# Weights of both half-steps in a permuted column order in SBUF, read back in order by TensorE, and split 512 columns at a time

## The chip, the cores and the metric

The kernel runs on one core of one Trainium2 chip. The metric is the device time of one execution in microseconds (us), shown as the median of the runs. A profiled execution has a span of its own, from its first to its last instruction. The core's engines work side by side, each through its own list of instructions: TensorE (PE; the loading of its stationary operand is shown apart as PEld), VectorE (DVE), ScalarE (ACT), GpSimd (POOL), and SyncE (SP), whose queue issues the loads of the weights.

## The reference, cut to what matters

One decoder layer for 256 tokens of 2048 features: a SwiGLU half-step, a mixer of three branches, a second SwiGLU half-step and a final norm, in float32.

```python
D_MODEL, SEQ, D_FF = 2048, 256, 5632

def swiglu(h, w_gate, w_up, w_down):
    return (jax.nn.silu(h @ w_gate) * (h @ w_up)) @ w_down

x = x + 0.5 * swiglu(rmsnorm(x, ffn1_norm[l]), ffn1_w_gate[l], ffn1_w_up[l], ffn1_w_down[l])
x = x + mixer(rmsnorm(x, mix_norm[l]), mem_n, ...)
x = x + 0.5 * swiglu(rmsnorm(x, ffn2_norm[l]), ffn2_w_gate[l], ffn2_w_up[l], ffn2_w_down[l])
return rmsnorm(x, final_norm)
```

w_gate and w_up are 2048 x 5632, w_down is 5632 x 2048. The mixer's weights lie between them in time.

## The kernel before, in words

Every matrix product with a weight goes through `gemm` (line 127). It makes a 128-token by 512-column result for each of the two blocks of tokens (`NB` = 2, `CW` = 512), and walks the rows of the weight in feature tiles of 128. `load` (line 106) brings four feature tiles with one DMA of 1 MB from the SP queue into a buffer `raw`, of which there are three. `split` (line 118) takes two of the four tiles at a time, 1024 columns in one instruction on each engine: ScalarE copies them, rounded to the type float32r, to `wh` (line 119), and VectorE subtracts `wh` from `raw` into `wl` (line 120), so that the two parts sum up to the weight. `wh` and `wl` have three buffers each. The activations are split in the same way (class `Split`). `products` (line 122) then issues three products for a feature tile and a block, into the same accumulator: high by high (line 123), high activation by low weight (line 124), low activation by high weight (line 125). In all three the activation is the stationary operand of 128 columns and the weight tile the moving operand, 512 columns of 4 bytes that lie one behind the other in SBUF.

Two feature tiles, called a pair below, are thus one split on each engine and 2 tiles x 2 blocks x 3 products = 12 products.

`ffn` (line 309) is a half-step. It works in two parts, of 6 and 5 chunks of 512 hidden features. A chunk is a `gemm` with w_gate over 16 feature tiles, a Silu on ScalarE, a `gemm` with w_up over 16 feature tiles, the product of both on VectorE, and its transposition and split (`tsplit`). Behind the chunks of a part come four `gemm`s with w_down, over 24 and over 20 feature tiles. `ffn` is called at line 402 for the first half-step and at line 784 for the second, with the mixer between them. In the very last `gemm` of the second half-step the last two groups of four tiles are split ahead into other buffers and taken block by block (`tail=2`).

Small pieces of other work (norms, masks, attention) are threaded between the products by `tick`. The order of the instructions on each engine is set by a scheduler that simulates a timeline of the program as it is built. Lines 653 and 654, in the mixer's linear attention, are VectorE subtractions on a view of 1024 columns cut in groups of 2m, of which one instruction takes the first m columns of each group and the other the last m, for m = 64, 32, 16, 8, 4, 2 and 1. One of their inputs is a single column of each group, repeated.

Of the kernel before, what the change touches and what calls it, by code (L numbers as in the profile page):

```python
# [8 lines left out]
F32 = mybir.dt.float32  # L9
# [4 lines left out]
ALU = mybir.AluOpType  # L14
AX = mybir.AxisListType
PSUM = bass.MemoryType.PSUM

P = 128
# [3 lines left out]
KT = D // P  # L22
DFF = 5632
CW = 512
NCH = D // CW
EPS = 1e-6
# [7 lines left out]


class Split:
    """A transposed activation [features, tokens] as two exact float32r parts, 8 feature tiles to a
    slot: x = high + low, each with at most 12 significant bits."""

    def __init__(self, new, n_tiles):  # L40
        n = (n_tiles + 7) // 8
# [18 lines left out]
def layer(ctx: ExitStack, tc: tile.TileContext, a: dict, out: bass.AP):  # L60
    nc = tc.nc
# [24 lines left out]
    x0 = a["x"][0]  # L86
    mem0 = a["mem"][0]

# [1 line left out]
    queue = []  # L90

    def tick(n=1):
# [9 lines left out]
        while queue and (gen is None or gen in queue):  # L102
            tick()

# [1 line left out]
    def load(w, row, col, parts=1):  # L106
        """Four feature tiles of a weight; parts: DMAs."""
        raw = wp.tile([P, 4, CW], F32, name="raw", tag="raw")
        n = 4 // parts
        for i in range(0, 4, n):  # L110
            r = row + i * P
            nc.sync.dma_start(
                raw[:, i : i + n, :],
                w[r : r + n * P, col : col + CW].rearrange("(j p) n -> p j n", p=P),
            )
        return raw

    def split(raw, wh, wl):
        nc.scalar.copy(wh, raw)  # L119
        nc.vector.tensor_tensor(wl, raw, wh.bitcast(F32), op=ALU.subtract)  # L120

    def products(lhs, kt, b, wh, wl, acc, first, last):
        nc.tensor.matmul(acc, lhsT=lhs.h(kt, b), rhs=wh, start=first, stop=False)  # L123
        nc.tensor.matmul(acc, lhsT=lhs.h(kt, b), rhs=wl, start=False, stop=False)  # L124
        nc.tensor.matmul(acc, lhsT=lhs.l(kt, b), rhs=wh, start=False, stop=last)  # L125

    def gemm(lhs, n_tiles, w, row0, col0, accs, ticks=0, raws=(), tail=0):
        """accs[b] = lhs of block b times a [n_tiles * P, CW] part of w. The last `tail` groups of
        four feature tiles go block by block, so that the first block is done early."""
        raws = list(raws)  # L130
        held = []
        for g0 in range(0, n_tiles, 4):
            raw = raws.pop(0) if raws else load(w, row0 + g0 * P, col0)
            late = g0 >= n_tiles - 4 * tail
            if late:
                both = [slot([P, 4, CW], F32R) for _ in range(2)]
                held.append((g0, *both))
            for h0 in (0, 2):
                if late:
                    wh, wl = (t[:, h0 : h0 + 2, :] for t in both)  # L140
                else:
                    wh = wp.tile([P, 2, CW], F32R, name="wh", tag="wh")
                    wl = wp.tile([P, 2, CW], F32R, name="wl", tag="wl")
                split(raw[:, h0 : h0 + 2, :], wh, wl)
                if late:
                    continue
                for b in range(NB):
                    for j in range(2):
                        kt = g0 + h0 + j
                        products(  # L150
                            lhs, kt, b, wh[:, j, :], wl[:, j, :], accs[b],
                            kt == 0, kt == n_tiles - 1,
                        )
                tick(ticks)
        for b in range(NB):
            for g0, wh, wl in held:
                for j in range(4):
                    kt = g0 + j
                    products(
                        lhs, kt, b, wh[:, j, :], wl[:, j, :], accs[b], kt == 0, kt == n_tiles - 1  # L160
                    )
# [12 lines left out]
        nc.scalar.copy(hi, ps)  # L174
        nc.vector.tensor_tensor(lo, ps, hi.bitcast(F32), op=ALU.subtract)  # L175

# [1 line left out]
    def square(src, ss, b, n):  # L178
        junk = tmp()
        nc.scalar.activation(junk, src, AF.Square, accum_out=ss[:, b, n : n + 1])  # L180
# [13 lines left out]
            )  # L194

    def rsqrt_mean(out_ap, sum_ap, n):
        """out = (sum / n + EPS) ** -0.5"""
        w = sum_ap.shape[1]
        t = sp.tile([P, 8], F32, name="rs", tag="rs")
        nc.vector.tensor_scalar(  # L200
            out=t[:, :w], in0=sum_ap, scalar1=1.0 / n, scalar2=EPS, op0=ALU.mult, op1=ALU.add
        )
        nc.gpsimd.tensor_tensor(out_ap, t[:, :w], mhalf[:, :w], op=ALU.pow)  # L203
# [9 lines left out]
            cp.tile([P, NB], F32, name=f"rs_{name}"),  # L213
        )

# [1 line left out]
    ident = cp.tile([P, P], F32, name="ident")  # L217
    make_identity(nc, ident)
    mhalf = cp.tile([P, 8], F32, name="mhalf")
# [10 lines left out]
        nc.tensor.transpose(out=ps[:, :n], in_=src, identity=ident[:n, :n])  # L230
        nc.vector.tensor_copy(gT[:, rows], ps[:, :n])

# [1 line left out]
    ss_m, rs_m = stats("m")  # L234
    mem_s = [slot([P, NB, 2 * CW]) for _ in range(2)]
    memT = Split(slot, KT)
# [4 lines left out]
    first = []  # L241
    for n in range(NCH):
        part = mem_s[n // 2][:, :, n % 2 * CW : (n % 2 + 1) * CW]
# [10 lines left out]
    xT = Split(slot, KT)  # L254
# [33 lines left out]
    for c in range(4):  # L288
        accs = [acc() for _ in range(NB)]
# [5 lines left out]
        for b in range(NB):  # L295
            r = rs_m[:, b : b + 1]
            if c < 2:
                t = tmp()
# [6 lines left out]
                )  # L305
    drain()

# [1 line left out]
    def ffn(xT, rs, wg, wu, wd, after, begin=lambda: None, final=False):  # L309
        done = 0  # L310
        for part, n_ch in enumerate((6, 5)):
            hT = Split(slot, 4 * n_ch)
            for c in range(n_ch):
                col = (done + c) * CW
                pg = [acc() for _ in range(NB)]
                gemm(xT, KT, wg, 0, col, pg, ticks=1)
                sil = [tmp() for _ in range(NB)]
                for b in range(NB):
                    nc.scalar.activation(sil[b], pg[b], AF.Silu, scale=rs[:, b : b + 1])  # L319
                pu = [acc() for _ in range(NB)]  # L320
                gemm(xT, KT, wu, 0, col, pu, ticks=1)
                for b in range(NB):
                    nc.vector.scalar_tensor_tensor(  # L323
                        out=sil[b], in0=pu[b], scalar=rs[:, b : b + 1], in1=sil[b],
                        op0=ALU.mult, op1=ALU.mult,
                    )
                    tsplit(sil[b], hT, 4 * c, b)
            if part == 1:
                begin()
            for n in range(NCH):  # L330
                pd = [acc() for _ in range(NB)]
                ends = final and part == 1 and n == NCH - 1
                gemm(
                    hT, 4 * n_ch, wd, done * CW, n * CW, pd, ticks=1, tail=2 if ends else 0
                )
                for b in range(NB):
                    xs = x_s[b][:, n * CW : (n + 1) * CW]
                    nc.vector.scalar_tensor_tensor(  # L338
                        out=xs, in0=pd[b], scalar=0.5, in1=xs, op0=ALU.mult, op1=ALU.add
                    )  # L340
                    if part == 1:
                        after(xs, b, n)
            done += n_ch
# [5 lines left out]
        nonlocal xT2  # L349
        xT2 = Split(slot, KT)  # L350

# [1 line left out]
    # acc[s, t] of a level m takes s in the first and t in the second half of a block of 2m.  # L353
    LEVELS = (64, 32, 16, 8, 4, 2, 1)
    masks = cp.tile([P, 8, P], U8, name="masks")
    tri = cp.tile([P, P], F32, name="tri")
# [3 lines left out]
    def prepare():  # L360
# [6 lines left out]
            out=masks[:, 7, :], in0=ix, scalar1=0, scalar2=None, op0=ALU.is_equal  # L367
        )
        yield
        at = tp.tile([P, 4, P], F32, name="at", tag="tmp")  # L370
        for i, m in enumerate(LEVELS):
            nc.vector.scalar_tensor_tensor(
                out=at[:, 0, :], in0=ix, scalar=m, in1=lt, op0=ALU.is_ge, op1=ALU.mult
            )
            nc.vector.scalar_tensor_tensor(
                out=masks[:, i, :], in0=ix, scalar=2 * m, in1=at[:, 0, :],
                op0=ALU.is_lt, op1=ALU.mult,
            )
        yield
        # Cumulative sums by a triangle, with GLA_TAU's exact 1/16.  # L380
        nc.gpsimd.memset(tri, 1.0 / 16.0)
        nc.gpsimd.affine_select(
            out=tri, in_=tri, pattern=[[1, P]], compare_op=ALU.is_ge, fill=0.0,
# [6 lines left out]
            out=ws, in_=ws, pattern=[[0, 4], [-1, P]], compare_op=ALU.is_ge, fill=0.0,  # L390
# [11 lines left out]
    def to_mixer(xs, b, n):  # L402
# [4 lines left out]
        xT, rs_1, a["ffn1_w_gate"][0], a["ffn1_w_up"][0], a["ffn1_w_down"][0],  # L407
        to_mixer,
        begin_mixer,
    )  # L410
    drain()
    for b in range(NB):
        rstd_of(ss_2, rs_2, b)

# [1 line left out]
    w_in = a["w_in"][0]  # L416
    rq = cp.tile([P, NB], F32, name="rq")
    nc.vector.tensor_scalar_mul(rq, rs_2, DK ** -0.5)
# [7 lines left out]
            for b in range(NB):  # L426
                leave(c, b, accs[b])

    # low-rank gate, [rank, tokens]
    glr = cp.tile([RANK, S], F32, name="glr")  # L430
    graw = tp.tile([P, KT, RANK], F32, name="graw", tag="tmp")
    nc.sync.dma_start(
# [16 lines left out]
                )  # L449
        nc.vector.tensor_copy(glr, pg[:RANK, :S])  # L450

    # spatial gating
    su = slot([P, NB, BW])
    sv = slot([P, NB, BW])

# [60 lines left out]

    queue.append(spatial())

    # cross-attention into the memory
    xqT = slot([P, 8, S])  # L520

    def to_T(dst_of, r):
# [58 lines left out]

    queue.append(attend())

    # gated linear attention
    qkT = slot([P, 2, HEADS, S])
    v_s = slot([P, NB, BW])
    r_s = slot([P, NB, BW])
    cum = slot([P, 2, HEADS, S])
    def log_decay():
        """cum[:, 0] = running sums of log_sigmoid(gate) / GLA_TAU over each 128 tokens, [d, h, t]"""  # L590
        zz = slot([P, 2, NB, CW])
        bias = tmp()
        bcast(bias, a["gla_gate_bias"][0])
# [10 lines left out]
        z, e = zz[:, 0], zz[:, 1]  # L604
# [21 lines left out]
    def linear_attention():  # L626
# [4 lines left out]
        c, e = cum[:, 0], cum[:, 1]  # L631
# [17 lines left out]
        for i, m in enumerate(LEVELS):  # L649
# [10 lines left out]
            yield  # L660
            level(qk[:, 0], qk[:, 1], i)
            yield
        # between the two blocks of 128
        mid = c[:, :, P - 1 : P].to_broadcast([P, HEADS, P])
        nc.vector.tensor_tensor(e[:, :, :P], mid, c[:, :, :P], op=ALU.subtract)
        nc.scalar.activation(e[:, :, :P], e[:, :, :P], AF.Exp)
# [53 lines left out]
    gla_gen = linear_attention()  # L720
    queue.append(gla_gen)

    # gates and branches
    merged = [slot([P, D]) for _ in range(NB)]
    w_br = a["w_branch"][0]
    for i in (1, 2, 0):
# [34 lines left out]
    for b in range(NB):  # L761
        rstd_of(ss_3, rs_3, b)

# [1 line left out]
    ss_4, rs_4 = stats("4")  # L765
    gf = slot([P, D])
    bcast(gf, a["final_norm"])
# [1 line left out]
    def last(xs, b, n):  # L769
# [12 lines left out]
            nc.sync.dma_start(out[0, b * P : (b + 1) * P, i * CW : (i + 1) * CW], xi)  # L782

    ffn(
        xT3, rs_3, a["ffn2_w_gate"][0], a["ffn2_w_up"][0], a["ffn2_w_down"][0], last, final=True
    )


# [29 lines left out]
```

## Time and profile before

| | |
|---|---|
| median of 2 runs | 2394.95 us (2394.32 to 2395.57) |
| span of the profiled execution | 2393.2 us |
| TensorE busy | 2373.6 us (99%), 10746 matmuls |
| VectorE busy | 1268.2 us (53%) |
| ScalarE busy | 1070.7 us (45%) |
| GpSimd busy | 58.4 us (2%) |
| DMA | 451.76 MB, mean 189 GB/s |

The span is the time of one profiled execution and is compared with another span; the median is that of the unprofiled runs. Matmuls are pipelined, so that the durations of neighbours overlap and a busy TensorE is not TensorE at its peak: what one costs is read from the distance of the starts.

### The profile page before, as it was taken

Reading aid. Unit: us, or ns where it says so; the run is one execution under the profiler, and the core shown is the slowest. Engines: PE = TensorE matmul, PEld = TensorE weight load, DVE = VectorE, ACT = ScalarE, POOL = GpSimd, SP = SyncE. Lnnn points to the kernel's source line nnn. Section 1 sums busy time; section 2 is a strip of 40 time slices with the busy share of each in tenths; the row PEclk is TensorE's granted clock in tenths of the full one; section 3 lists DMA queues with packets and bytes.
Section 4 is the critical chain, followed back from the end, with each engine's and each line's share of the span. In section 5 each row is a group of like instructions: output and inputs, shape, how many; then the busy total and the mean of one; then the engine's idle time right before and its main releaser. Section 6 shows DMA issues by size and latency. Waiting matters only on the chain.

```text
span 2393.2 us, 26429 instructions
## 1 busy us (share of the span) xinstructions
PE 2373.6 (99%) x10746; PEld 1962.7 (82%) x10746; DVE 1268.2 (53%) x1330; ACT 1070.7 (45%) x1265; POOL 58.4 (2%) x56
## 2 busy tenths in 40 slices
PE   8999999999999999999999999999999999999998
PEld 6888888888888878888788888888888888888887
DVE  5644545445545545556765555555454454454454
ACT  6544444344444444435444444445444433444443
POOL 0000000000000001000200000000000000000000
PEclk9999999999999999999999999999999999999999
DMA  7555555566556665445556555555556555556654
GB/s 261 184 191 187 186 193 193 194 193 191 180 192 202 203 195 178 157 163 167 165 164 216 193 194 189 199 192 183 188 192 194 188 188 194 192 187 193 193 189 146
DMA packets 226227, 451.76 MB, mean 189 GB/s; under 512 B 9316, under 2 KB 9384, under 8 KB 225464
## 3 DMA queue, kind: packets, MB, share of 16 engines
q1 hardware_dynamic: 224408, 442.69, 57.0%
q0 software_dynamic: 1696, 7.37, 0.8%
q8 instruction: 84, 1.38, 0.2%
q14 instruction: 39, 0.32, 0.0%
HBM read 445.84 MB, written 4.19 MB: 188 GB/s over the span
## 4 chain that ended last, share of the span: by engine, by line
PE 96%; DVE 1%; ACT 1%; issue 1%; DMA 1%; SPq 0%; ACTq 0%; POOLq 0%; POOL 0%; DVEq 0%
PE acc L124 31%; PE acc L125 31%; PE acc L123 31%; PE trp L166 2%; DVE wl L120 1%; PE sml L638 0%; DMA graw<-in_w_in_dram 0%; PE sml L543 0%; PE sml L571 0%; ACT wh L119 0%; PE sml L446 0%; DMA m<-in_mem_dram 0%; ACT m L655 0%; ACT tmp L180 0%; PE sml L692 0%
## 5 line engine op out<-in xcount | busy, mean ns | idle before, releaser
L120 DVE TENSOR_TENSOR wl<-raw,wh 128x1024 fp32r<-128x1024 f32 x828 | 1028.6, 1243 | 1025.1 <-ACT wh L119 1024.9
L119 ACT CAST wh<-raw 128x1024 fp32r<-128x1024 f32 x828 | 871.3, 1053 | 1158.9 <-PE acc L125 1142.8
L124 PE MATMUL acc<-wl,m 128*128 128x512 f32 x3312 | 1294.9, 391 | 1.9 <-DVE wl L120 1.7
L125 PE MATMUL acc<-wh,m 128*128 128x512 f32 x3312 | 1291.3, 390 | 0.1
L123 PE MATMUL acc<-wh,m 128*128 128x512 f32 x3312 | 1185.8, 392 | 3.5 <-ACT wh L119 2.5
L123 PEld LDWEIGHTS acc<-wh,m 128*128 128x128 f32 x3312 | 622.3, 188 | 133.3 <-ACT wh L119 3.7
L124 PEld LDWEIGHTS acc<-wl,m 128*128 128x128 f32 x3312 | 622.9, 188 | 132.2 <-DVE wl L120 3.6
L125 PEld LDWEIGHTS acc<-wh,m 128*128 128x128 f32 x3312 | 622.5, 188 | 128.1 <-DVE m L191 0.5
L190 ACT ACTIVATE m<-trp,gT 128x128 fp32r<-128x128 f32 x128 | 42.8, 363 | 23.9 <-PE trp L166 14.3
L174 ACT CAST m<-trp 128x512 fp32r<-128x512 f32 x64 | 34.9, 588 | 40.9 <-PE trp L166 40.9
L175 DVE TENSOR_TENSOR m<-trp,m 128x512 fp32r<-128x512 f32 x64 | 41.7, 685 | 21.2 <-ACT m L174 20.9
L191 DVE SCALAR_TENSOR_TENSOR m<-trp,gT,m 128x128 fp32r<-128x128 f32 x128 | 41.1, 346 | 14.3 <-ACT m L190 13.5
L166 PEld LDWEIGHTS trp<-ident,tmp 128*128 128x128 f32 x288 | 34.7, 140 | 6.6
L166 PE MATMUL trp<-ident,tmp 128*128 128x128 f32 x288 | 40.0, 272 | 0.0
L319 ACT ACTIVATE tmp<-acc,rs 128x512 f32<-128x512 f32 x44 | 30.1, 690 | 19.5 <-PE acc L125 19.5
L180 ACT ACTIVATE tmp<-m 128x512 f32<-128x512 f32 x40 | 24.8, 624 | 15.6 <-DVE m L338 11.9
L323 DVE SCALAR_TENSOR_TENSOR tmp<-acc,rs,tmp 128x512 f32<-128x512 f32 x44 | 30.9, 743 | 0.0
L166 PE MATMUL trp<-ident,m 128*128 128x128 f32 x160 | 22.8, 280 | 3.0 <-DMA m<-in_mem_dram 3.0
L338 DVE SCALAR_TENSOR_TENSOR m<-acc,m 128x512 f32<-128x512 f32 x32 | 20.6, 682 | 9.5 <-PE acc L125 9.5
L203 POOL TENSOR_TENSOR rs<-rs,mhalf 128x1 f32<-128x1 f32 x8 | 4.3, 552 | 868.6 <-DVE rs L200 868.6
L166 PEld LDWEIGHTS trp<-ident,m 128*128 128x128 f32 x160 | 19.7, 145 | 6.7 <-DMA m<-in_mem_dram 3.1
L658 POOL TENSOR_TENSOR m<-m,m 128x1024 f32<-128x1024 f32 x7 | 20.9, 2990 | 115.4 <-ACT m L655 88.2
(135 smaller groups left out, 387.3 us busy)
## 6 DMA issues: line engine op xcount, KB each, us to landing
raw<-in_w_in_dram SPq DMA_DIRECT2D x96, 1024.0 KB, 5.0
raw<-in_ffn_w_gate_dram SPq DMA_DIRECT2D x88, 1024.0 KB, 5.2
raw<-in_ffn_w_up_dram SPq DMA_DIRECT2D x88, 1024.0 KB, 5.2
raw<-in_ffn_w_down_dram SPq DMA_DIRECT2D x88, 1024.0 KB, 5.1
raw<-in_w_branch_dram SPq DMA_DIRECT2D x24, 1024.0 KB, 5.1
raw<-in_w_out_dram SPq DMA_DIRECT2D x16, 1024.0 KB, 5.1
raw<-in_w_kv_mem_dram SPq DMA_DIRECT2D x14, 1024.0 KB, 5.1
m<-in_mem_dram SPq DMA_DIRECT2D x4, 512.0 KB, 8.3
```

What stands on the lines that cost most here:

```text
L119: nc.scalar.copy(wh, raw)
L120: nc.vector.tensor_tensor(wl, raw, wh.bitcast(F32), op=ALU.subtract)
L123: nc.tensor.matmul(acc, lhsT=lhs.h(kt, b), rhs=wh, start=first, stop=False)
L124: nc.tensor.matmul(acc, lhsT=lhs.h(kt, b), rhs=wl, start=False, stop=False)
L125: nc.tensor.matmul(acc, lhsT=lhs.l(kt, b), rhs=wh, start=False, stop=last)
L166: nc.tensor.transpose(out=ps[:, j * P : (j + 1) * P], in_=src[:, j * P : (j + 1) * P], identity=ident)
L174: nc.scalar.copy(hi, ps)
L175: nc.vector.tensor_tensor(lo, ps, hi.bitcast(F32), op=ALU.subtract)
L190: nc.scalar.activation(dst.h(kt, b), pj, AF.Copy, scale=g)
L191: nc.vector.scalar_tensor_tensor(out=dst.l(kt, b), in0=pj, scalar=g, in1=dst.h(kt, b).bitcast(F32), op0=ALU.mult, op1=ALU.subtract,)
L319: nc.scalar.activation(sil[b], pg[b], AF.Silu, scale=rs[:, b : b + 1])
L323: nc.vector.scalar_tensor_tensor(out=sil[b], in0=pu[b], scalar=rs[:, b : b + 1], in1=sil[b], op0=ALU.mult, op1=ALU.mult,)
```

## The change

The two calls of `ffn` get three run lengths each: e = 2, 4 and 16 columns for w_gate, w_up and w_down of the first half-step, 32, 64 and 8 for those of the second. For these weights the 512 columns of a feature tile lie in SBUF in another order. A group of 2e columns is cut in two; its first e columns go to the first half of the tile's row (256 columns, 1 KB), its last e columns to the second half, and the next group follows behind. ScalarE and VectorE write `wh` and `wl` through that view, one feature tile (512 columns) per instruction instead of two, and TensorE reads the moving operand through the same view, which gives the columns back in their own order: e columns of one half, e of the other, the next e of the first half, and so on. `raw` is read in order. All other products, the mixer's and the tail's, stay as they were, and so do all loads.

```diff
+    def laid(t, e):
+        if e is None:
+            return t
+        return t.rearrange("p (h c e) -> p c h e", h=2, e=e)
+
-    def split(raw, wh, wl):
-        nc.scalar.copy(wh, raw)
-        nc.vector.tensor_tensor(wl, raw, wh.bitcast(F32), op=ALU.subtract)
+    def split(raw, wh, wl, e=None):
+        if e is None:
+            nc.scalar.copy(wh, raw)
+            nc.vector.tensor_tensor(wl, raw, wh.bitcast(F32), op=ALU.subtract)
+            return
+        for j in range(raw.shape[1]):
+            r = raw[:, j, :].rearrange("p (c h e) -> p c h e", h=2, e=e)
+            hi, lo = laid(wh[:, j, :], e), laid(wl[:, j, :], e)
+            nc.scalar.copy(hi, r)
+            nc.vector.tensor_tensor(lo, r, hi.bitcast(F32), op=ALU.subtract)
...
-                split(raw[:, h0 : h0 + 2, :], wh, wl)
+                split(raw[:, h0 : h0 + 2, :], wh, wl, None if late else e)
...
-                            lhs, kt, b, wh[:, j, :], wl[:, j, :], accs[b],
+                            lhs, kt, b, laid(wh[:, j, :], e), laid(wl[:, j, :], e), accs[b],
...
-                gemm(xT, KT, wg, 0, col, pg, ticks=1)
+                gemm(xT, KT, wg, 0, col, pg, ticks=1, e=runs[0])
...
-                gemm(xT, KT, wu, 0, col, pu, ticks=1)
+                gemm(xT, KT, wu, 0, col, pu, ticks=1, e=runs[1])
...
+                    e=runs[2],
...
+        runs=(2, 4, 16),
...
+        runs=(32, 64, 8),
```

The instructions on ScalarE where the first w_gate chunk of the first half-step ends and its w_up chunk has begun, before (`wh` and `raw` with their buffer numbers):

```order
L119 CAST wh_1131<-raw_1129 128x1024
L119 CAST wh_1147<-raw_1129 128x1024
L119 CAST wh_1171<-raw_1169 128x1024
L119 CAST wh_1187<-raw_1169 128x1024
L319 ACT_TABLE_LOAD
L319 ACTIVATE tmp_1163<-acc_989,rs_1_219 128x512
L319 ACTIVATE tmp_1164<-acc_990,rs_1_219 128x512
L119 CAST wh_1205<-raw_1203 128x1024
```

The same place in the changed kernel, where line 133 is the copy of 512 columns, "128x128x2x2" is 128 partitions by 128 groups of two runs of 2, and "x2" stands for two instructions:

```order
L133 CAST wh_1143<-raw_1141 128x128x2x2 x2
L133 CAST wh_1161<-raw_1141 128x128x2x2 x2
L133 CAST wh_1187<-raw_1185 128x64x2x4 x2
L133 CAST wh_1205<-raw_1185 128x64x2x4 x2
L333 ACT_TABLE_LOAD
L333 ACTIVATE tmp_1179<-acc_989,rs_1_219 128x512
L333 ACTIVATE tmp_1180<-acc_990,rs_1_219 128x512
L133 CAST wh_1225<-raw_1223 128x64x2x4 x2
```

Each copy has become two of half the columns, and the Silu (line 319, now 333) stands at the same place between them; VectorE's subtractions change in the same way.

TensorE in the next w_gate chunk, where the transposes (line 166) of the chunk before come between the products, before:

```order
L123 MATMUL acc_1321<-wh_1341,m8_220 128x512
L124 MATMUL acc_1321<-wl_1342,m8_220 128x512
L125 MATMUL acc_1321<-wh_1341,m8_222 128x512
L124 MATMUL acc_1322<-wl_1342,m8_220 128x512
L125 MATMUL acc_1322<-wh_1341,m8_222 128x512
L166 MATMUL trp_1306<-ident_79,tmp_1163 128x128 x4
L166 MATMUL trp_1314<-ident_79,tmp_1164 128x128 x4
L123 MATMUL acc_1322<-wh_1341,m8_220 128x512
```

And in the changed kernel, where lines 137, 138 and 139 are the three products and line 180 the transposes:

```order
L137 MATMUL acc_1353<-wh_1375,m8_220 128x512
L138 MATMUL acc_1353<-wl_1376,m8_220 128x512
L139 MATMUL acc_1353<-wh_1375,m8_222 128x512
L138 MATMUL acc_1354<-wl_1376,m8_220 128x512
L180 MATMUL trp_1338<-ident_79,tmp_1179 128x128 x4
L180 MATMUL trp_1346<-ident_79,tmp_1180 128x128 x4
L139 MATMUL acc_1354<-wh_1375,m8_222 128x512
L137 MATMUL acc_1354<-wh_1375,m8_220 128x512
```

The transposes have moved ahead of one product; the number and the width of the products are unchanged.

## Rows read from the trace of the kernel before

**Rows 1.** Page, section 1: the span, and busy time of each engine.

```profile
span 2393.2 us, 26429 instructions
PE 2373.6 (99%) x10746; PEld 1962.7 (82%) x10746; DVE 1268.2 (53%) x1330; ACT 1070.7 (45%) x1265; POOL 58.4 (2%) x56
```

**Rows 2.** Page, section 4: chain that ended last, shares by engine and by line.

```profile
PE 96%; DVE 1%; ACT 1%; issue 1%; DMA 1%; SPq 0%; ACTq 0%; POOLq 0%; POOL 0%; DVEq 0%
PE acc L124 31%; PE acc L125 31%; PE acc L123 31%; PE trp L166 2%; DVE wl L120 1%; PE sml L638 0%; DMA graw<-in_w_in_dram 0%; PE sml L543 0%; PE sml L571 0%; ACT wh L119 0%; PE sml L446 0%; DMA m<-in_mem_dram 0%; ACT m L655 0%; ACT tmp L180 0%; PE sml L692 0%
```

**Rows 3.** Grouped lines: operation, shapes, count, busy us, mean ns, idle before, releasers.

```profile
L124 PE MATMUL acc<-wl,m 128*128 128x512 f32 x3312 | 1294.9, 391 | 1.9 <-DVE wl L120 1.7
L125 PE MATMUL acc<-wh,m 128*128 128x512 f32 x3312 | 1291.3, 390 | 0.1
L123 PE MATMUL acc<-wh,m 128*128 128x512 f32 x3312 | 1185.8, 392 | 3.5 <-ACT wh L119 2.5 <-ACT m L190 0.8
L120 DVE TENSOR_TENSOR wl<-raw,wh 128x1024 fp32r<-128x1024 f32 x828 | 1028.6, 1243 | 1025.1 <-ACT wh L119 1024.9
L119 ACT CAST wh<-raw 128x1024 fp32r<-128x1024 f32 x828 | 871.3, 1053 | 1158.9 <-PE acc L125 1142.8 <-issue 12.7 <-ACT m L190 1.0
...
L175 DVE TENSOR_TENSOR m<-trp,m 128x512 fp32r<-128x512 f32 x64 | 41.7, 685 | 21.2 <-ACT m L174 20.9
...
L174 ACT CAST m<-trp 128x512 fp32r<-128x512 f32 x64 | 34.9, 588 | 40.9 <-PE trp L166 40.9
...
L125 PE MATMUL acc<-m,m 128*128 128x512 f32 x16 | 6.2, 389 | 0.0
```

**Rows 4.** Timeline of TensorE, 600 to 606 us: start, duration, operation.

```profile
600.76 0.39 PE L123 MATMUL acc<-wh,m 128*128 128x512 f32 x1
...
603.49 0.39 PE L123 MATMUL acc<-wh,m 128*128 128x512 f32 x1
...
605.98 0.39 PE L125 MATMUL acc<-wh,m 128*128 128x512 f32 x1
```

**Rows 5.** Windows: stretch, length, busy us by engine, granted clock, DMA share, GB/s.

```profile
core 0: us, PE busy (x) PEld busy (x) DVE busy (x) ACT busy (x) POOL busy (x), PEclk, DMA share, GB/s
107.00:486.00 379.00, 379.00 (x1699) 314.35 (x1698) 187.65 (x168) 161.39 (x165) 0.00 (x0) 1.00 0.59 189
...
2032.00:2380.00 348.00, 348.00 (x1558) 288.55 (x1557) 176.18 (x161) 148.02 (x159) 0.00 (x0) 1.00 0.57 184
```

**Rows 6.** Waits: who waited for whom, us in total, times, longest us.

```profile
ACT wh L119 <- PE acc L125: 1142.8, 705, 3.8
...
PE acc L123 <- ACT wh L119: 2.5, 3, 1.7
PE acc L124 <- DVE wl L120: 1.7, 3, 0.9
```

**Rows 7.** Page, section 6: DMA issues, count, KB each, median us to landing.

```profile
raw<-in_ffn_w_gate_dram SPq DMA_DIRECT2D x88, 1024.0 KB, 5.2
...
raw<-in_ffn_w_down_dram SPq DMA_DIRECT2D x88, 1024.0 KB, 5.1
```

**Rows 8.** Timelines of ScalarE and VectorE, 603 to 608 us; in brackets idle time.

```profile
603.68 1.05 ACT L119 CAST wh<-raw 128x1024 fp32r<-128x1024 f32 x1 [1.66 <-PE acc L125]
606.40 1.05 ACT L119 CAST wh<-raw 128x1024 fp32r<-128x1024 f32 x1 [1.67 <-PE acc L125]
...
604.77 1.23 DVE L120 TENSOR_TENSOR wl<-raw,wh 128x1024 fp32r<-128x1024 f32 x1 [1.50 <-ACT wh L119]
```

**Rows 9.** Lines 653 and 654: durations min/median/max in ns, first and last start.

```profile
L653 DVE TENSOR_TENSOR m<-m x7: 678/681/693, 1091.4 to 1198.0; 128x512 f32<-128x512 f32 x7
...
L654 DVE TENSOR_TENSOR m<-m x7: 676/683/686, 1092.0 to 1199.8; 128x512 f32<-128x512 f32 x7
```

**Rows 10.** Timeline of TensorE around line 617, a product of unrounded f32.

```profile
1088.14 1.95 PE L617 MATMUL sml<-tri,m 128*128 128x128 f32 x16
1089.84 0.48 PE L124 MATMUL acc<-wl,m 128*128 128x512 f32 x1
```

More of the change, by code (lines that the diff above doesn't have):

```diff
@@ L125, in products, with gemm @@
         nc.tensor.matmul(acc, lhsT=lhs.l(kt, b), rhs=wh, start=False, stop=last)
-    def gemm(lhs, n_tiles, w, row0, col0, accs, ticks=0, raws=(), tail=0):
+    def gemm(lhs, n_tiles, w, row0, col0, accs, ticks=0, raws=(), tail=0, e=None):
         raws = list(raws)
@@ L306, in layer, with ffn @@
     drain()
-    def ffn(xT, rs, wg, wu, wd, after, begin=lambda: None, final=False):
+    def ffn(xT, rs, wg, wu, wd, after, begin=lambda: None, final=False, runs=(None, None, None)):
         done = 0
@@ L333, in ffn @@
                 gemm(
-                    hT, 4 * n_ch, wd, done * CW, n * CW, pd, ticks=1, tail=2 if ends else 0
+                    hT, 4 * n_ch, wd, done * CW, n * CW, pd, ticks=1, tail=2 if ends else 0,
+                    e=runs[2],
                 )
@@ L784, in layer @@
     ffn(
-        xT3, rs_3, a["ffn2_w_gate"][0], a["ffn2_w_up"][0], a["ffn2_w_down"][0], last, final=True
+        xT3, rs_3, a["ffn2_w_gate"][0], a["ffn2_w_up"][0], a["ffn2_w_down"][0], last, final=True,
+        runs=(32, 64, 8),
     )
```

## The prediction

> **What bounds the kernel now.** I read the page's busy line first: TensorE is busy for 99% of a span of 2393.2 us, VectorE for 53% and ScalarE for 45% [rows 1]. The chain of waits says the same from the other end: 96% of it is TensorE, and three lines, the three products of a split weight, hold 31% each [rows 2]. The grouped lines then give the counts: 3312 instructions on each of these lines, each 512 columns wide, plus 48 in the tail [rows 3]. Their mean of about 390 ns is no price, since they overlap; the price is the spacing of their starts. In the timeline twelve products (one pair of feature tiles, both blocks) go from 600.76 to 603.49 us and 23 of them from 600.76 to 605.98, so one costs 5.22 / 23 = 227 ns, or 0.443 ns a column [rows 4]. [...] Nobody keeps TensorE waiting: it waited 2.5 us in all for ScalarE's wh and 1.7 us for VectorE's wl, while ScalarE waited 1142.8 us for TensorE to give buffers back [rows 6]. So the time follows the spacing of the products, and anything that only burdens the other engines must first use up their idle time.
>
> **What the change does, part by part.**
>
> *Count.* Each half-step has 88 / 2 = 44 loads of each of its three weights [rows 7] (the row of w_up, left out there, reads like that of w_gate); a load is two pairs of feature tiles, so 88 pairs and 88 x 12 = 1056 products for each weight (48 fewer for the last one, whose tail stays as it was). The six weights get runs of e = 2, 4, 16 columns in the first half-step and 32, 64, 8 in the second.
>
> *Splits of 512 columns.* 6 x 88 - 4 = 524 pairs are now split by two instructions on each engine. ScalarE: the 1024-column copy takes 1053 ns, and the nearest 512-column one 588 ns; VectorE: 1243 ns, and 685 ns [rows 3]. A pair then costs 2 x 588 = 1176 ns instead of 1053 on ScalarE and 2 x 685 = 1370 ns instead of 1243 on VectorE: 524 x 123 = 64 us and 524 x 127 = 67 us more work. A pair comes round every 2.72 us, and in it ScalarE idles for 1.67 and VectorE for 1.50 us [rows 8]. That idle time hides both; without it the two sums would be the price. The products wait for no more than before, and the first half of wh is ready sooner. I take 0. The order on TensorE changes only where single products or transposes swap places, which costs nothing while its queue is full.
>
> *Split writes and reads in short runs.* VectorE already does this: lines 653 and 654 each walk 512 of 1024 columns in runs of 64, 32, 16, 8, 4, 2 and 1 with a gap as long as the run, on one input and the output, and all fourteen take between 676 and 693 ns [rows 9]. Runs of 2 are therefore free for VectorE, as far as hops of some bytes stand for hops of 1 KB. For ScalarE no row has such runs. The bounds: nothing, or a doubled price for each column. From 512 to 1024 columns its copy grows by 465 ns, so doubling adds that to each 512: 2 x 1053 = 2106 ns for a pair, still under 2720. If VectorE's halves doubled whole, 2740 ns would pass 2720 by a hair: 88 pairs x some 0.2 us with the work at a chunk's end, under 20 us. I take 0, by the VectorE rows.
>
> *TensorE's reads.* The only term that is not hidden. A product reads 512 columns of wh or wl; now they come as 512 / e runs, taken in turn from the two halves of a 2 KB row. No moving operand of the old kernel is read in runs below 128 columns, so the trace has no row for it. The lower bound is 0 (VectorE's rows: runs of 2 cost nothing there). But TensorE is more pressed: 0.443 ns a column against 685 / 512 = 1.34 ns on VectorE, so 8 adjacent bytes last it 0.89 ns and VectorE 2.7 ns. Whether a pair of columns can be fetched in 0.89 ns from an address that jumps each time is the whole question. [...] For half speed there are two prices. Twice the spacing is 454 ns, 227 more. The nearest slower row of TensorE is line 617: 16 products of 128 columns between 1088.14 and 1089.84 us, 106 ns each, 0.83 ns a column [rows 10]; 512 such columns make 425 ns, 198 more. (Those operands are unrounded f32, so it is a neighbour, not the same thing.) I take the middle, 212 ns: 1056 x 212 = 224 us, with 209 and 239 us at the ends. A gain I exclude: shorter runs cannot beat reading in order, unless today's reading meets some conflict, for which no row speaks.
>
> [...]
>
> **The sum.** 0 + 0 + 224 us on the profiled span of 2393.2 gives 2617; the median shown, 2394.95, lies 1.75 us over that span [rows 1], so 2619 us.
>
> **The rivals.**
>
> *A, reads in order cost nothing from any address:* not slower, 2395 us (2394 to 2400 with leftovers at chunk starts). Place: the 1056 products on ffn1's w_gate. For it speaks that VectorE's fourteen calls do not feel run length at all [rows 9]; against it that TensorE asks for its columns three times as fast. It decides up to 48 us / 1056 = 45 ns for one product: below that the change can't be told from none. [...]
>
> *B, my forecast:* only e = 2 falls to half speed, 2619 us.
>
> *C, longer runs pay too.* Either e = 4 also runs at half speed (a fetch must bring 8 columns): twice the term, 2395 + 448 = 2843 us, or each hop costs the same 212 / 256 = 0.83 ns: (256 + 128 + 32 + 16 + 8 + 64) = 504 hops, 504 x 0.83 x 1056 ns = 442 us, 2837 us. For it speaks that no row shows what a hop of 1 KB costs; against the second that VectorE with 512 hops in 512 columns shows none [rows 9].
>
> *D, e = 2 pays in part,* because fetches overlap: half of the term, 112 us, 2507 us.
>
> *E, ScalarE or VectorE becomes the bound,* priced above: under 20 us and within A, unless a split more than doubles.
>
> **How the numbers follow.** B 0.38, A (with E) 0.35, C 0.15, D 0.10, faster 0.02. [...] The likeliest is 2619 us, its own range 2600 to 2640. A, D and B together are 0.83, so the range goes from 2390 (A) to 2720 (B with up to 45% of the same loss on e = 4); what is left out is most of C. About 2% of 2395, 48 us, is what a measurement of this kernel can tell from no change: slower B, C and nearly all of D, 0.62; same 0.36; faster 0.02.
>
> **What would show it.** In the timeline of the first half-step's w_gate chunks the starts of products should lie 425 to 454 ns apart, and a chunk's 96 products should take 42 us instead of 21.8; with A, 227 ns. In w_up of the same half-step and in all three weights of the second, 227 ns in any case but C. The granted clock stays at 1.00. The split lines show 1048 instructions each, means near 590 and 690 ns whatever e is, and TensorE's waits for wh and wl stay at a few us. I am wrong if the w_gate stretch keeps its 227 ns (A), if the w_up stretch grows as well (C), or if TensorE begins to wait for the splits by tens of us (E).

## The result, and the profile after

The changed kernel takes 2568.88 us (median of 2 runs, 2568.63 to 2569.13) against 2394.95: a ratio of 1.0729, 95% interval 1.0712 to 1.0747. It is 173.9 us slower. The profiled executions differ by as much, 2566.9 against 2393.2 us.

The page of the changed kernel: its span, its busy times and the granted clock of TensorE in 40 slices:

```profile
span 2566.9 us, 27477 instructions
...
PE 2548.7 (99%) x10746; PEld 1978.1 (77%) x10746; DVE 1307.1 (51%) x1854; ACT 1124.5 (44%) x1789; POOL 58.4 (2%) x56
...
PEclk9999999999999999999999999999999999999999
```

TensorE is the bound as before [rows 1, 2], with the same 10746 matmuls, the same granted clock (0.999 in the mean, 0.998 before), and 175 us more of busy time. The grouped lines, which answer to [rows 3] (137 to 139 are the three products, 133 and 134 the halved splits):

```profile
L138 PE MATMUL acc<-wl,m 128*128 128x512 f32 x3312 | 1358.7, 411 | 1.9 <-DVE wl L128 1.8
L139 PE MATMUL acc<-wh,m 128*128 128x512 f32 x3312 | 1356.4, 410 | 0.1
...
L134 DVE TENSOR_TENSOR wl<-raw,wh 128x512 fp32r<-128x512 f32 x1048 | 678.7, 689 | 805.3 <-ACT wh L133 803.8
...
L133 ACT CAST wh<-raw 128x512 fp32r<-128x512 f32 x1048 | 605.7, 626 | 870.6 <-PE acc L139 859.8
```

The products got longer and nothing waits for anything new: the idle time ahead of line 138 is 1.9 us, as it was, ScalarE still waits for TensorE, and VectorE for ScalarE. So the time went into the products themselves. The timeline of TensorE in the changed kernel, one stretch for each run length, in the order of the program: w_gate (e = 2), w_up (4) and w_down (16) of the first half-step, w_up (64), w_gate (32) and w_down (8) of the second:

```profile
190.99 0.51 PE L137 MATMUL acc<-wh,m 128*128 128x512 f32 x1
...
193.32 0.51 PE L139 MATMUL acc<-wh,m 128*128 128x512 f32 x1
...
204.41 0.42 PE L139 MATMUL acc<-wh,m 128*128 128x512 f32 x1
204.67 0.41 PE L137 MATMUL acc<-wh,m 128*128 128x512 f32 x1
204.91 0.42 PE L138 MATMUL acc<-wl,m 128*128 128x512 f32 x1
...
459.69 0.40 PE L137 MATMUL acc<-wh,m 128*128 128x512 f32 x1
...
460.89 0.40 PE L139 MATMUL acc<-wh,m 128*128 128x512 f32 x1
...
1840.03 0.39 PE L137 MATMUL acc<-wh,m 128*128 128x512 f32 x1
...
1841.16 0.39 PE L137 MATMUL acc<-wh,m 128*128 128x512 f32 x1
...
1861.64 0.40 PE L137 MATMUL acc<-wh,m 128*128 128x512 f32 x1
1861.88 0.40 PE L138 MATMUL acc<-wl,m 128*128 128x512 f32 x1
1862.11 0.40 PE L139 MATMUL acc<-wh,m 128*128 128x512 f32 x1
...
2100.54 0.41 PE L137 MATMUL acc<-wh,m 128*128 128x512 f32 x1
...
2101.27 0.65 PE L137 MATMUL acc<-wh,m 128*128 128x512 f32 x2
```

Seven steps from 190.99 to 193.32 us make 333 ns for e = 2. With e = 4 the steps alternate, 0.26 and 0.24 us, 250 ns in the mean. Five steps from 459.69 to 460.89 make 240 ns for e = 16, five from 1840.03 to 1841.16 make 226 for e = 64, the steps of 0.24 and 0.23 at 1861.64 some 236 for e = 32, and three from 2100.54 to 2101.27 make 243 for e = 8. In order it was 227 [rows 4]. Over all products of each weight the mean step is 332, 250, 240, 237, 227 and 243 ns; times 1056 products the six differences, 105 + 23 + 13 + 10 + 0 + 16 = 167 ns, make 176 us, which covers the loss of 173.7 us between the two spans.

### The profile page after: what moved, and what is told of

Same layout as the page of the kernel before. It is cut to its first block, busy times and chain, and to the rows that moved or that the text cites. A ratio compares the mean times of both kernels' runs of the same rounds, so it can differ in the third digit from the quotient of the medians.

```text
span 2566.9 us, 27477 instructions
## 1 busy us (share of the span) xinstructions
PE 2548.7 (99%) x10746; PEld 1978.1 (77%) x10746; DVE 1307.1 (51%) x1854; ACT 1124.5 (44%) x1789; POOL 58.4 (2%) x56
## 4 chain that ended last, share of the span: by engine, by line
PE 97%; DVE 1%; issue 1%; ACT 1%; DMA 1%; ACTq 0%; POOLq 0%; POOL 0%; SPq 0%; DVEq 0%
PE acc L138 31%; PE acc L139 31%; PE acc L137 31%; PE trp L180 2%; PE sml L654 0%; DVE wl L128 0%; DMA graw<-in_w_in_dram 0%; PE sml L559 0%; PE sml L587 0%; PE sml L462 0%; ACT wh L127 0%; ACT m L671 0%; DMA m<-in_mem_dram 0%; ACT tmp L194 0%; PE sml L708 0%
## 5 line engine op out<-in xcount | busy, mean ns | idle before, releaser
L138 PE MATMUL acc<-wl,m 128*128 128x512 f32 x3312 | 1358.7, 411 | 1.9 <-DVE wl L128 1.8
L139 PE MATMUL acc<-wh,m 128*128 128x512 f32 x3312 | 1356.4, 410 | 0.1
L137 PE MATMUL acc<-wh,m 128*128 128x512 f32 x3312 | 1247.6, 411 | 2.3 <-ACT wh L127 1.3
L134 DVE TENSOR_TENSOR wl<-raw,wh 128x512 fp32r<-128x512 f32 x1048 | 678.7, 689 | 805.3 <-ACT wh L133 803.8
L133 ACT CAST wh<-raw 128x512 fp32r<-128x512 f32 x1048 | 605.7, 626 | 870.6 <-PE acc L139 859.8
L128 DVE TENSOR_TENSOR wl<-raw,wh 128x1024 fp32r<-128x1024 f32 x304 | 387.0, 1274 | 332.1 <-ACT wh L127 332.0
L127 ACT CAST wh<-raw 128x1024 fp32r<-128x1024 f32 x304 | 319.0, 1051 | 395.7 <-PE acc L139 386.0
```

Of the source, the lines that this page charges most:

```text
L133: nc.scalar.copy(hi, r)
L134: nc.vector.tensor_tensor(lo, r, hi.bitcast(F32), op=ALU.subtract)
```

## The experiments

Theory R at the start: the cost lies in TensorE's reading and depends on the run length of the read alone. Rival W: it comes from the short-run writes or the doubled number of splits. In the diffs below `+` and `-` stand against the changed kernel, if nothing else is said. In all of its variants but the one with blocks, the two views take the number of parts of a row beside the run length: the changed kernel's own runs then read ((2, 2), (2, 4), (2, 16)) and ((2, 32), (2, 64), (2, 8)), which changes nothing by itself.

**Reads alone.**

```diff
-                split(raw[:, h0 : h0 + 2, :], wh, wl, None if late else e)
+                split(raw[:, h0 : h0 + 2, :], wh, wl)
```

> TensorE reads through the six run lengths (2, 4, 16; 32, 64, 8) as in the changed kernel, but ScalarE and VectorE split 1024 columns at a time in plain order, so the columns that the six products see are in another order (that part of the computation is changed). Theory R, the cost lies in TensorE's reads alone: all of the changed kernel's loss, 2560 to 2575 us, starts of products 333 ns apart in the e = 2 weight, 250 in e = 4, 243 in e = 8, 240 in e = 16, 237 in e = 32, 227 in e = 64. Rival W, the loss comes from the short-run writes or the halved splits meeting TensorE's reads in SBUF: about 2395 us, 227 ns everywhere.

Measured: 2567.81 us, ratio 1.0726 (1.0708 to 1.0744), steps of 331, 250, 240, 237, 227 and 243 ns: the whole loss, with plain writes and 1024-column splits. Its split on ScalarE, and TensorE in the weight with e = 2 (four steps, 333 ns each):

```profile
L127 ACT CAST wh<-raw 128x1024 fp32r<-128x1024 f32 x828 | 872.9, 1055 | 1306.1 <-PE acc L139 1276.7 <-issue 13.3 <-DVE m L353 13.1
```

```profile
190.49 0.51 PE L138 MATMUL acc<-wl,m 128*128 128x512 f32 x1
...
191.82 0.51 PE L139 MATMUL acc<-wh,m 128*128 128x512 f32 x1
```

**Writes alone.**

```diff
-                            lhs, kt, b, laid(wh[:, j, :], e), laid(wl[:, j, :], e), accs[b],
+                            lhs, kt, b, wh[:, j, :], wl[:, j, :], accs[b],
```

> The splits of 512 columns are written in the six run lengths as in the changed kernel, but TensorE reads each row in plain order, so the columns that the six products see are in another order (that part of the computation is changed). Theory R: within 0.3% of before, 2390 to 2400 us, products 227 ns apart everywhere; ScalarE and VectorE carry the 1048 halved splits in their idle time. Rival W: up to 2569 us.

Measured: 2395.1 us, ratio 1.0001 (0.9992 to 1.0010). Its page and its waits of TensorE:

```profile
PE 2373.7 (99%) x10746; PEld 1962.6 (82%) x10746; DVE 1307.7 (55%) x1854; ACT 1127.0 (47%) x1789; POOL 58.4 (2%) x56
```

```profile
PE acc L137 <- ACT wh L127: 2.7, 3, 1.8
...
PE acc L138 <- DVE wl L128: 1.8, 3, 0.9
```

The halved splits cost VectorE 39.5 us and ScalarE 56 us more [rows 1] and the kernel nothing. W has fallen. Within the e = 2 weight of the changed kernel the step is also the same whether ScalarE and VectorE are both idle in the middle of it (mean 332.5 ns, 481 products) or both busy (331 ns, 131 products).

**One weight alone, and a run length that is free.** Against the changed kernel:

```diff
-        runs=(2, 4, 16),
+        runs=((2, 2), None, None),
...
-        runs=(32, 64, 8),
+        runs=(None, None, None),
```

> Only w_gate of the first half-step keeps its runs of 2; the other five weights are laid, split and read as before. If each weight pays for itself (333 against 227 ns for 1056 products): 2395 + 112 = 2507 us, 2500 to 2513, 65% of the loss. The forecast's half speed for e = 2 would be 2619 us, which the trace of the changed kernel already excludes; if the weights disturbed each other (buffers, queues), it would be nearer to 2569 or to 2395.

Measured: 2504.8 us, 110 us more than before (ratio 1.0463, 1.0447 to 1.0479). The weight pays for itself, and it pays half of what I had forecast.

```diff
+        runs=((2, 64), (2, 64), (2, 64)),
...
+        runs=((2, 64), (2, 64), (2, 64)),
```

> All six weights get runs of 64 (256 bytes), whose products stood 227 ns apart in the second half-step's w_up. If a run of 64 with a hop of 1 KB is free whatever the weight: same as before, 2393 to 2398 us. If the 227 ns came from that weight's place in the program and not from its runs: some weights at 230 to 240 ns and 2410 to 2450 us.

Measured: 2394.45 us, ratio 1.0000 (0.9991 to 1.0009), 227 ns in all six weights. Runs of 64 columns (256 bytes) from two halves are free in every weight.

**What a hop costs.** That the cost lies in the reading is settled, but not why 2 columns cost 105 ns and 16 columns 13, nor that the run length alone decides. In the next four kernels the row is cut into more parts than two, which shortens the hops at the same run length. The view in `laid` changes, the one of the split's input in the same way, and the runs with them, now as (parts, run length):

```diff
-        return t.rearrange("p (h c e) -> p c h e", h=2, e=e)
+        return t.rearrange("p (h c e) -> p c h e", h=e[0], e=e[1])
...
-        runs=(2, 4, 16),
+        runs=((4, 2), (8, 2), (16, 2)),
...
-        runs=(32, 64, 8),
+        runs=((32, 2), (64, 2), (128, 2)),
```

> Runs of 2 in all six weights, with the row cut in 4, 8, 16 parts (first half-step: gate, up, down) and 32, 64, 128 parts (second), so that a hop is 512, 256, 128, 64, 32 and 16 bytes instead of 1 KB. Theory J (each jump of the address stops TensorE's reading for a fixed time): 333 ns between products in all six, 3 x 106 + ... = 6 x 1056 x 106 ns = 672 us more than before, 3065 us. Theory L (what counts is whether the next columns lie in something already fetched): 333 ns or more for the long hops and falling to 227 for the 16 or 32 byte hops. Theory D (the two places of 1 KB distance collide in one bank): other than 333 at most distances, some at 227.

```diff
+        runs=((4, 4), (8, 4), (16, 4)),
...
+        runs=((32, 4), (64, 4), (2, 128)),
```

> Runs of 4 with hops of 512, 256, 128 bytes (first half-step) and 64, 32 bytes (second, gate and up), and runs of 128 with a hop of 1 KB (second, down). Theory J: 250 ns at every distance, since 250 was measured at 1 KB, and 227 in the runs of 128. Theory L: 250 or below, 227 for the short hops. Theory D: distances differ both ways, some over 250.

```diff
+        runs=((4, 8), (8, 8), (16, 8)),
...
+        runs=((32, 8), (2, 1), (256, 1)),
```

> Runs of 8 with hops of 512, 256, 128 bytes (first half-step) and 64 bytes (second, gate); single columns that alternate between two halves 1 KB apart (second, up); single columns in steps of 8 bytes (second, down, which passes over the row twice). Theory J: 243 ns for the runs of 8; for single columns at 1 KB, one stop for each of 512 hops: 227 + 512 x 0.415 = 440 ns. Theory L: single columns at 1 KB pay as much as pairs, 333, if the pair's cost was the second place and not the hop, and steps of 8 bytes at least as much as pairs, 333, since half of everything fetched is unused.

```diff
+        runs=((4, 16), (8, 16), (16, 16)),
...
+        runs=((4, 32), (8, 32), (4, 64)),
```

> Runs of 16 with hops of 512, 256, 128 bytes (first half-step), runs of 32 with hops of 512 and 256 bytes and runs of 64 with a hop of 512 bytes (second). Theory J: 240 ns for all three with runs of 16, 237 for runs of 32, 227 for runs of 64. Theory D: values that change with the distance.

They took 3842.94, 2515.97, 2647.4 and 2443.54 us (one run each, before 2393.69 beside them). Median step between products in ns, by run length and number of parts (the mean for runs of 4 and 8 in 2 parts, where the steps alternate); the first column is the changed kernel's layout, and most of the row of single columns comes from a later kernel:

| run | 2 parts, 1 KB | 4, 512 B | 8, 256 B | 16, 128 B | 32, 64 B | 64, 32 B | 128, 16 B |
|---|---|---|---|---|---|---|---|
| 1 | 216 | 283 | 487 | 435 | 433 | 431 | 461 |
| 2 | 333 | 443 | 487 | 473 | 431 | 460 | 451 |
| 4 | 250 | 269 | 279 | 247 | 225 | 233 | |
| 8 | 243 | 231 | 246 | 230 | 232 | | |
| 16 | 240 | 232 | 239 | 241 | | | |
| 32 | 236 | 233 | 236 | | | | |
| 64 | 227 | 227 | | | | | |
| 128 | 227 | | | | | | |

So the distance of the hop counts as well as the run length: R in its strict form is out. TensorE in the kernel with pairs, in the weight cut into 4 parts, where nine steps make 443 ns each:

```profile
209.86 0.64 PE L137 MATMUL acc<-wh,m 128*128 128x512 f32 x1
...
213.85 0.64 PE L137 MATMUL acc<-wh,m 128*128 128x512 f32 x1
```

Two rows stand out. The timeline of TensorE in the kernel with single columns, at the weight that alternates between two halves 1 KB apart, and behind it at the weight read in steps of 8 bytes:

```profile
1717.67 0.38 PE L138 MATMUL acc<-wl,m 128*128 128x512 f32 x1
...
1719.40 0.38 PE L139 MATMUL acc<-wh,m 128*128 128x512 f32 x1
...
1961.44 0.65 PE L138 MATMUL acc<-wl,m 128*128 128x512 f32 x1
...
1965.06 0.63 PE L137 MATMUL acc<-wh,m 128*128 128x512 f32 x1
```

Eight steps from 1717.67 to 1719.40 make 216 ns: hopping 1 KB at every single column is *faster* than reading in order. Eight from 1961.44 to 1965.06 make 452 ns, twice the price in order. So a fixed price for a hop (J) is out: 512 hops cost less than none, and 256 hops cost between 105 and 260 ns by their distance. L, which the expectation set beside it, is out too, since pairs with hops of 32 and 16 bytes took 460 and 451 ns where it wants 227; and no distance gives the pairs the 227 ns that D wants at some. The pairs from four and more parts run at 431 to 487 ns: here is the half speed that the forecast expected of two parts.

**What is carried on, as theory S.** It says no more than these numbers do: 512 single columns taken by turns from two places take 216 ns, where 512 in order take 227 and 512 in steps of 8 bytes 452. Why that is so, no run shows. 216 ns is also the shortest mean step of such a product in any run. S was made from these numbers, one weight at one distance, so the next two kernels are its test. For more than two places it says nothing; a guess from the table is that single columns repeat the steps of pairs from half as many parts, 333, 443, 487, 473, 431 and 460 ns, 1265 ns more than six times 227: 2394 + 1056 x 1265 ns = 3730 us.

```diff
+        runs=((4, 1), (8, 1), (16, 1)),
...
+        runs=((32, 1), (64, 1), (128, 1)),
```

> Single columns taken in turn from 4, 8 and 16 parts of a row (first half-step: gate, up, down) and 32, 64, 128 parts (second). [...] Rival J (a fixed stop at each jump, with single columns exempt): 216 in all.

Measured: 3615.7 us (one run); 283, 487, 435, 433, 431 and 461 ns, the rest of the first row of the table. At the weight cut into 4 parts six steps make 283 ns each:

```profile
119.68 0.45 PE L137 MATMUL acc<-wh,m 128*128 128x512 f32 x1
...
121.38 0.45 PE L137 MATMUL acc<-wh,m 128*128 128x512 f32 x1
```

With 64 and 128 parts they repeat the pairs from half as many parts within 1 ns, with 8, 16 and 32 parts they are 8 to 11% off, with 4 parts 15% (283 for 333); J, which wants 216 in all, is out. What gained from two places loses from four and more, 56 to 260 ns against reading in order. Why the steps change so with the number of the parts, and why runs of 4 to 32 lose up to 52 ns, no run tells.

In the second test the two places stand closer together. By S all six weights run at 216 ns, 10.8 under the price in order before rounding: 2394 - 6 x 1056 x 10.8 ns = 2326 us.

```diff
-        return t.rearrange("p (h c e) -> p c h e", h=2, e=e)
+        return t.rearrange("p (g h c) -> p g c h", h=2, c=e)
...
-            r = raw[:, j, :].rearrange("p (c h e) -> p c h e", h=2, e=e)
+            r = raw[:, j, :].rearrange("p (g c h) -> p g c h", h=2, c=e)
...
-        runs=(2, 4, 16),
+        runs=(4, 8, 16),
...
-        runs=(32, 64, 8),
+        runs=(32, 64, 128),
```

> Single columns in turn from two neighbouring blocks of 4, 8, 16 columns (first half-step: gate, up, down) and 32, 64, 128 columns (second), so that the two places read in turn lie 16, 32, 64, 128, 256 and 512 bytes apart instead of 1 KB. [...] Rival: 216 needs the 1 KB distance, 227 or more at the small ones.

Measured: 2329.22 us (one run), 216 ns in all six weights, from 16 bytes to 512 between the two places. This is what S says, and already faster than both kernels. Seven steps at a distance of 16 bytes:

```profile
119.67 0.38 PE L138 MATMUL acc<-wl,m 128*128 128x512 f32 x1
...
121.18 0.38 PE L138 MATMUL acc<-wl,m 128*128 128x512 f32 x1
```

But the grouped lines of this kernel show a price that the pairs had not:

```profile
L133 ACT CAST wh<-raw 128x512 fp32r<-128x512 f32 x1048 | 1093.5, 1165 | 214.9 <-PE acc L139 214.9
L134 DVE TENSOR_TENSOR wl<-raw,wh 128x512 fp32r<-128x512 f32 x1048 | 1092.6, 1132 | 210.7 <-ACT wh L133 210.3
```

Writing single columns takes ScalarE 1165 ns for 512 columns and VectorE 1132, against 626 and 689 when most runs were longer. It is not the single column as such that costs this: in the kernel above that read one weight in steps of 8 bytes, that weight was also written so, and there ScalarE took 665 ns in the mean of 168 splits and VectorE 699. Two of them:

```profile
1989.64 0.65 ACT L133 CAST wh<-raw 128x512 fp32r<-128x512 f32 x1 [4.21 <-PE acc L139]
...
1984.91 0.69 DVE L134 TENSOR_TENSOR wl<-raw,wh 128x512 fp32r<-128x512 f32 x1 [4.12 <-ACT wh L133]
```

So columns that go by turns to two places, 16 to 512 bytes apart, are slow to write (1165 and 1132 ns in the mean), and columns in steps of 8 bytes are not.

**The gain for every weight, twice.** First with permuted writes, where S gives 216 instead of 227 ns for 9936 products, 10.8 x 9936 = 107 us less, 2288 us. Against the kernel before:

```diff
-    def split(raw, wh, wl):
+    def split(raw, wh, wl, plain=False):
+        if not plain:
+            raw = raw.rearrange("p j (c h) -> p j c h", h=2)
+            wh, wl = (t.rearrange("p j (h c) -> p j c h", h=2) for t in (wh, wl))
...
+    def woven(t):
+        return t.rearrange("p (h c) -> p c h", h=2)
...
-                            lhs, kt, b, wh[:, j, :], wl[:, j, :], accs[b],
+                            lhs, kt, b, woven(wh[:, j, :]), woven(wl[:, j, :]), accs[b],
```

> Built on the kernel before: every split weight of the whole kernel (tail apart) lies in two halves, even columns in the first and odd ones in the second half of a row of 512, and TensorE reads single columns from the two halves in turn; splits stay 1024 columns wide. [...] Rival: the 216 ns of the single columns belongs to that weight's place in the program, or the single-column writes hold up ScalarE and VectorE: 2380 us and more.

Measured: 2364.51 us, ratio 0.9876 (0.9859 to 0.9892). The products stand 216 ns apart, but less than a third of the gain arrives. Grouped lines and waits of TensorE:

```profile
L123 DVE TENSOR_TENSOR wl<-raw,wh 128x1024 fp32r<-128x1024 f32 x828 | 1798.3, 2190 | 313.1 <-ACT wh L122 310.7
L122 ACT CAST wh<-raw 128x1024 fp32r<-128x1024 f32 x828 | 1768.0, 2148 | 313.9 <-PE acc L131 309.8 <-ACT wh L122 0.7 <-DVE tmp L329 0.6
```

```profile
PE acc L130 <- DVE wl L123: 42.8, 39, 3.1
PE acc L129 <- ACT wh L122: 6.1, 5, 2.6
```

A pair now comes every 12 x 0.216 = 2.59 us, of which VectorE needs 2.19 and ScalarE 2.15 for the split alone. Of the starts that came more than 20 ns late behind a product, TensorE lost 90 us in this kernel, 31 before 200 us and 51 between 700 and 1700 us, around and in the mixer; from 200 to 700 and from 1700 to 2200 us, in the half-steps, it lost under 2. There the engines bear the slow writes, as they did in the kernel with blocks, which had them in the half-steps alone and lost hardly more to late starts than the kernel before (25 and 20 us).

Then with plain writes: the products take the columns woven, so the accumulator holds them in another order, and whoever empties it reads every second column. Against the kernel before, one of the 11 places (the expectation counts 12):

```diff
     def products(lhs, kt, b, wh, wl, acc, first, last):
+        wh, wl = woven(wh), woven(wl)
...
+    def plain(t):
+        return t.rearrange("p (c h) -> p h c", h=2)
...
-                    nc.scalar.activation(sil[b], pg[b], AF.Silu, scale=rs[:, b : b + 1])
+                    nc.scalar.activation(two(sil[b]), plain(pg[b]), AF.Silu, scale=rs[:, b : b + 1])
```

(`two` gives the other operand the same shape, its columns staying in order.)

> Built on the kernel before: the splits stay as they were (1024 columns, plain order), TensorE takes single columns from the first and the second half of each row in turn for all 9984 products, and the order is set right where the results leave PSUM (the 12 places that read an accumulator read every second column). Theory S with free writes: 216 instead of 227 ns for 9984 products, 10.9 x 9984 = 109 us less, 2286 us (2280 to 2292), no waits for wh and wl. It also tells what held the version with permuted writes back at 2364 us: if its single-column writes did (2148 and 2190 ns for 1024 columns instead of 1053 and 1243), this one has ScalarE at 1050 and VectorE at 1240 ns and loses none of the gain; if something else at 216 ns did, this one stays near 2364 us as well. Rival for the accumulators: reading every second column of PSUM doubles the 200 or so operations that empty them (0.7 to 1.4 us each), which the four accumulators hide, at most some 10 us at the ends.

Measured: 2285.9 us (5 runs, 2285.03 to 2286.81), ratio 0.9545 (0.9531 to 0.9558): 108.7 us faster than the kernel before. Its page, grouped lines and timeline:

```profile
span 2285.1 us, 26420 instructions
...
PE 2261.1 (99%) x10746; PEld 1975.1 (86%) x10746; DVE 1268.8 (56%) x1330; ACT 1065.5 (47%) x1265; POOL 58.1 (3%) x56
```

```profile
L120 DVE TENSOR_TENSOR wl<-raw,wh 128x1024 fp32r<-128x1024 f32 x828 | 1029.1, 1244 | 923.0 <-ACT wh L119 921.7
L119 ACT CAST wh<-raw 128x1024 fp32r<-128x1024 f32 x828 | 866.6, 1047 | 1060.6 <-PE acc L135 1048.2 <-ACT m L200 9.5 <-issue 1.3
...
L333 DVE SCALAR_TENSOR_TENSOR tmp<-acc,rs,tmp 128x512 f32<-128x512 f32 x44 | 30.9, 744 | 0.0
L329 ACT ACTIVATE tmp<-acc,rs 128x512 f32<-128x512 f32 x44 | 30.0, 687 | 17.1 <-PE acc L135 17.1
```

```profile
301.00 0.38 PE L133 MATMUL acc<-wh,m 128*128 128x512 f32 x1
...
302.73 0.59 PE L133 MATMUL acc<-wh,m 128*128 128x512 f32 x2
```

Eight steps from 301.00 to 302.73 us are 216 ns. The splits are back at 1047 and 1244 ns [rows 3] and the late starts at 23 us, which shows that the single-column writes had held the other version back. The Silu that reads every second column of PSUM takes 687 ns (line 329), and VectorE's product 744 (line 333). The same two lines in the kernel before, which read in order:

```profile
L323 DVE SCALAR_TENSOR_TENSOR tmp<-acc,rs,tmp 128x512 f32<-128x512 f32 x44 | 30.9, 743 | 0.0
L319 ACT ACTIVATE tmp<-acc,rs 128x512 f32<-128x512 f32 x44 | 30.1, 690 | 19.5 <-PE acc L125 19.5
```

Nothing doubled, so the rival for the accumulators is out as well. Every second column is a step of 8 bytes, the step that was free for writes too (699 and 665 ns for 512 columns).

## Why the prediction was right, and where it was not

*What bounds, and the two zeros: right.* TensorE's spacing alone set the time. Splits of 512 columns and short-run writes cost 0 (the kernel with writes alone: 1.0001); the halves took 626 and 689 ns, where 588 and 685 had been taken from [rows 3], and the idle time of [rows 8] covered them. VectorE's rows with short runs [rows 9] were a good guide for VectorE in runs of 2 and more. Their single columns lie in steps of 8 bytes, so they did not tell of single columns written by turns to two places (1132 ns). ScalarE, for which no row had short runs, paid a little for runs of 2: 662 ns in the mean against 617 to 620 for the longer ones.

*The term of TensorE's reads: right in place and sign, wrong in size, twice.* The range and the direction held (2569 in 2390 to 2720), the likeliest time did not: 2619 with its own range of 2600 to 2640 was 50 us too high. The step that failed is the price of e = 2: 212 ns taken, 105 measured, so 111 us instead of 224. No run shows the 212 ns for pairs from two halves, an estimate between twice the spacing and the spacing of line 617 [rows 10]. That part went as rival D (half of the term), whose time would have been 2507 and is what the weight alone gave, 2504.8 us. D's reason, that fetches overlap, was not put to a test. The second is the zero for runs of 4 and more, which from two halves no run shows for runs under 64: runs of 4, 8, 16 and 32 lose 23, 16, 13 and 10 ns, together 62 x 1056 ns = 65 us. That was rival C's place, and C's sign, a w_up stretch that grows, did show (250 ns), but not by C's mechanism: one price for each hop would have made e = 4 lose half as much as e = 2 and e = 64 something. Two errors of opposite sign put 2569 between D and B, so that the range held is in part luck: it was wide enough to reach from A to beyond B, and no rival in it had this sum of terms.

*The half speed behind B* was the author's estimate, and part of the runs show it. With four or more parts pairs do run at 431 to 487 ns, where the forecast's two prices were 425 and 454. That line 617 [rows 10] comes near them may be chance: its moving operands are read in order. With two parts the pairs ran at 333 ns, and single columns from two places at 216, faster than pairs and than reading in order; why was not shown. The differences by distance (225 to 279 ns for runs of 4), and what runs of 4 to 32 lose, stay open too.

*"A gain I exclude":* wrong, and the costliest sentence of the prediction. It left one way out, "unless today's reading meets some conflict, for which no row speaks". There was something: reading in order is itself 11 ns slower than woven reading, 227 against 216, in 9984 products, 109 us. The 0.443 ns a column of [rows 4] could not tell this by itself, since the faster 216 / 512 = 0.422 came only with the experiments; but that no row speaks for a gain did not say that there is none.

## What to carry to other kernels

When TensorE is the bound, do not take the spacing of its products in order for the shortest that it can reach: here weaving the columns from two places of a row took 11 of 227 ns away and 4.5% of the time, by views alone, with the order set right where the accumulators are emptied. Of moving operands of 4 bytes, runs of 64 columns were free at the hops tried, 512 bytes and 1 KB (227 ns), runs of 4 to 32 lost up to 52 ns of 227, and pairs 105 to 260 ns. Single columns gained from two places alone, 11 ns: from four and more they lost 56 to 260. Put a permutation where the engine is not pressed, and look at its steps: reading PSUM in steps of 8 bytes cost nothing (744 and 687 ns against 743 and 690), and writing single columns of SBUF by turns to two places nearly doubled the splits (2190 and 2148 ns against 1244 and 1047). Since writes in steps of 8 bytes were free as well (699 and 665 ns for 512 columns), the step and not the side may be what counts; a split that reads `raw` in steps of 8 bytes and writes each half in order was not tried.

## What the runs showed of the hardware

- Reading the moving operand one column at a time from two places, 16 bytes to 1 KB apart, ran at 216 ns for 512 columns, in order at 227, in steps of 8 bytes at 452. From four parts and more single columns took 283 to 487 ns.
- VectorE wrote runs of 2 as fast as longer ones (in the changed kernel 690 ns for 512 columns against 688 to 689), ScalarE nearly so (662 against 617 to 620). Single columns that go by turns to two halves of a row took 2190 and 2148 ns for 1024 columns instead of 1244 and 1047; single columns in steps of 8 bytes took 699 and 665 ns for 512.
- Both read every second column of PSUM, in steps of 8 bytes, as fast as all in order: 744 and 687 ns for 512 columns, where the same two lines took 743 and 690 in order in the kernel before.
